# Differential attention in an encoder trunk: the score products over 64 rows each, three per component, in place of two over 128 rows

## The chip, the cores and the metric

The kernel runs on one core of a Trainium2 chip, in one launch. The metric is the device time of that core in microseconds, as the median of several executions. One more execution was taken with the hardware profiler; its trace is what is read below.

## The reference

Two layers over 512 tokens with 1024 channels, all in float32. Each layer normalizes x, multiplies it by one large input matrix and feeds two mixers: a differential attention and a gated linear recurrence (HGRN2, both directions). Their outputs are projected, gated, added, projected again and added to x; a SwiGLU block follows. What the change touches is the attention's scores:

```
def diff_attention(h_q, h_k, h_v, cos, sin, lam, norm_gain, layer):
    q = h_q.reshape(B, S, DA_HEADS, 2, DA_QK_DIM)      # 4 heads, 2 components, 64 channels
    k = h_k.reshape(B, S, DA_HEADS, 2, DA_QK_DIM)
    v = h_v.reshape(B, S, DA_HEADS, DA_V_DIM)          # 128 channels
    ...                                                # partial rotary on q and k
    def block(qi):                                     # 128 queries
        s = jnp.einsum('bqhcd,bkhcd->bhcqk', qi, k).astype(jnp.float32)
        p = jax.nn.softmax(s, axis=-1)
        w = p[:, :, 0] - lam_full * p[:, :, 1]
        return jnp.einsum('bhqk,bkhv->bqhv', w.astype(v.dtype), v)
```

So each head has two score matrices, one per component c, each a product over only 64 channels.

## The kernel before

**Precision by splitting.** Nearly every product on TensorE takes operands of type F32R, and each float32 operand x is made into two of them: hi, a copy of x cast to F32R, and lo, the rest x - hi. `split_act` (L91-92) does this with a ScalarE copy (recorded at L92) and a VectorE subtraction (recorded at L81, the line of the helper `tt`). A product is then summed from three: hi·hi, hi·lo, lo·hi (`mm3`, L209-212). Activations (helper `act`) are recorded at L78, scalar_tensor_tensor at L84.

**Stages of a layer** (L723 on): projections for the recurrence with the recurrence itself (`hgrn_head`), projections for queries (`aq`), keys (`ak`) and values, attention (L629), the second half of the gate `gb`, the projection of the recurrence's output by w_b, the gate `ga`, then the projection of the attention's output by w_a (which reads `oah`, `oal`, written by the attention), the one by w_o, and the feed-forward block. Projections run through `project_fm` and `project_tm`: weights come in by DMA (`raw`), are split into `hi` and `lo`, and 24 products (12 where the depth is 512) fill one accumulator `m`.

**Attention.** Loops over 4 heads, and in each over 4 tiles of 128 queries (`todo`, L695). Per head, `operands` (L633) turns the queries and keys by 4 + 4 TensorE transposes (L640) into the accumulators `qkt`, channels on partitions: component 0 on partitions 0 to 63, component 1 on 64 to 127. From there it makes three operands for both components:

- `q2[:, c, :]`: the hi part of component c on its own 64 partitions, the lo part on the other 64;
- `ka[:, c, :]`: the same for the keys;
- `kb[:, c, :]`: the keys with the halves exchanged, lo on the component's own partitions and hi (a cast copy) on the other.

In the profile, `q2` has the name q. That is six copies on ScalarE (L649, L652) and six subtractions on VectorE (L650, L653, recorded at L81) of 64 partitions by 512 each, a copy and a subtraction by turns, for the subtraction reads what the copy wrote.

Per tile, `exps` (L656) then needs two products per component over all 128 partitions: q2·ka gives hi·hi + lo·lo, q2·kb gives hi·lo + lo·hi (L664, L667; four products of 128x512, one accumulator `qk` per component). VectorE takes the maximum of each (L669), ScalarE the exponential with its sum (L670, recorded at L78). `weights` (L673) joins both components to one weight tile, which TensorE turns (L714, `wt`) and `split_act` splits into `wh` and `wl`. At the end of a head, `values` multiplies by the values (`ao`) and `finish` normalizes and writes `oah`, `oal`.

**What sets the order.** The program says what depends on what, and a planner in the framework lays out one fixed order per engine: where an instruction of the attention isn't ready, TensorE gets a product of a later projection instead. `urgent()` puts weight loads, splits and evacuations first. `behind(a, b)` (L94) is an order without a wait: a is placed after b in the plan. In `exps`, the first product of a head's first tile is placed behind the last subtraction of `operands` (L665). Operand tiles have one buffer each, score and side accumulators share four banks (`bank`, L107), projections have four of their own (`mbank`, L110).

Of the kernel before, what the change touches and what calls it, by code (L numbers as in the profile page):

```python
# [9 lines left out]
F32 = mybir.dt.float32  # L10
F32R = mybir.dt.float32r
# [3 lines left out]
ALU = mybir.AluOpType  # L15
# [3 lines left out]
P = 128  # L19
D = 1024  # L20
DC = D // P
T = 512
# [25 lines left out]
def kernel(  # L48
# [17 lines left out]
    PE, DVE, ACT, POOL = nc.tensor, nc.vector, nc.scalar, nc.gpsimd  # L66
# [13 lines left out]
    def tt(o, a, b, op):  # L80
        return DVE.tensor_tensor(o, a, b, op)  # L81
# [9 lines left out]
    def split_act(src, hi, lo):  # L91
        return ACT.copy(hi, src), tt(lo, src, hi.bitcast(F32), ALU.subtract)  # L92

    def behind(ins, other):  # L94

        tc.add_manual_dep(ins.ins, other.ins.name,
                          mybir.DependencyInfo(mybir.DependencyClass.NoSync, mybir.DependencyReason.DATA),
                          reason="keep the tensor engine from waiting")
# [46 lines left out]
    hl = cp.tile([P, DC, T], F32R, tag="hl", name="hl")  # L145
# [121 lines left out]
    with tc.tile_pool(name="init", bufs=1, reuse_waits="tile") as ip:  # L267
# [41 lines left out]
        with tc.issue_after(norms[-1][1].ins):  # L309
# [56 lines left out]
            for dst, quarter in ((sin, 0.0), (cos, 0.25)):  # L366
                n = ip.tile([P, 32], F32, tag="n", name="n")
# [261 lines left out]
    def attention(l, aq, ak, avh, avl, oh, ol, ap):  # L629

        def operands(h):  # L633

            half = [slice(0, 64), slice(64, 128)]
            turned = []
            for src in (aq, ak):
                pt = bank("qkt")
                for t in range(TC):
                    PE.transpose(pt[:, t * P:(t + 1) * P], src[:, t, h * P:(h + 1) * P], ident)  # L640
                turned.append(pt)
            q2 = ap.tile([P, 2, T], F32R, tag="q2", name="q2", bufs=1)
            ka = ap.tile([P, 2, T], F32R, tag="ka", name="ka", bufs=1)
            kb = ap.tile([P, 2, T], F32R, tag="kb", name="kb", bufs=1)
            for pt, dst, swapped in ((turned[0], q2, None), (turned[1], ka, kb)):
                for c in range(2):
                    own, other = half[c], half[1 - c]
                    hi = dst[own, c, :]
                    ACT.copy(hi, pt[own, :])  # L649
                    mark = tt(dst[other, c, :], pt[own, :], hi.bitcast(F32), ALU.subtract)  # L650
                    if swapped is not None:
                        ACT.copy(swapped[other, c, :], pt[own, :])  # L652
                        mark = tt(swapped[own, c, :], pt[own, :], hi.bitcast(F32), ALU.subtract)  # L653
            return (q2, ka, kb), mark

        def exps(q2, ka, kb, t, mark):  # L656

            tok = slice(t * P, (t + 1) * P)
            nm = sm.tile([P, 2], F32, tag="nm", name="nm")
            den = sm.tile([P, 2], F32, tag="den", name="den")  # L660
            e = ap.tile([P, 2, T], F32, tag="e", name="e", bufs=2)
            ps = [bank("qk") for c in range(2)]
            for c in range(2):
                mm = PE.matmul(ps[c], q2[:, c, tok], ka[:, c, :], start=True, stop=False)  # L664
                if t == 0 and c == 0:  # L665
                    behind(mm, mark)
                PE.matmul(ps[c], q2[:, c, tok], kb[:, c, :], start=False, stop=True)  # L667
            for c in range(2):
                DVE.tensor_reduce(nm[:, c:c + 1], ps[c], AX.X, ALU.max, negate=True)  # L669
                mark = act(e[:, c, :], ps[c], AF.Exp, bias=nm[:, c:c + 1], accum=den[:, c:c + 1])  # L670
            return e, den, mark

        def weights(e, den):  # L673
            DVE.reciprocal(den, den)
            tt(den, den, dcoef[:, l, :], ALU.mult)
            tsc(e[:, 1, :], e[:, 1, :], den[:, 1:2], None, ALU.mult)
            return stt(e[:, 0, :], e[:, 0, :], den[:, 0:1], e[:, 1, :], ALU.mult, ALU.add)

        def values(h, wh, wl, mark):
            po = bank("ao")  # L680
            hc = slice(h * P, (h + 1) * P)
            for s in range(TC):
                if s == 0 and mark is not None:
                    behind(PE.matmul(po, avh[:, s, hc], wh[:, s, :], start=True, stop=False), mark)
                    PE.matmul(po, avh[:, s, hc], wl[:, s, :], start=False, stop=False)
                    PE.matmul(po, avl[:, s, hc], wh[:, s, :], start=False, stop=False)
                else:
                    mm3(po, avh[:, s, hc], avl[:, s, hc], wh[:, s, :], wl[:, s, :], s == 0, s == TC - 1)
            return head_squares(po)[0]

        def finish(h, parts, mark):
            o = head_norm(*parts, dgain[:, 4 * l + h:4 * l + h + 1], mark)
            split_act(o, oh[:, h, :], ol[:, h, :])

        todo = [(h, t) for h in range(HEADS) for t in range(TC)]  # L695
        ops, mark = operands(0)
        e, den, _ = exps(*ops, 0, mark)
        for n, (h, t) in enumerate(todo):
            mark = weights(e, den)
            if t == 0:  # L700
                if h:
                    parts = values(h - 1, wh, wl, mark)
                wh = ap.tile([P, TC, T], F32R, tag="wh", name="wh", bufs=1)
                wl = ap.tile([P, TC, T], F32R, tag="wl", name="wl", bufs=1)
            elif t == 1 and h:
                finish(h - 1, parts, mark)
            w, mark = e, None
            if n + 1 < len(todo):
                if t == TC - 1:
                    ops, mark = operands(h + 1)  # L710
                e, den, mark = exps(*ops, todo[n + 1][1], mark)
            pt = bank("wt")
            for s in range(TC):
                tr = PE.transpose(pt[:, s * P:(s + 1) * P], w[:, 0, s * P:(s + 1) * P], ident)  # L714
                if mark is not None:
                    behind(tr, mark)
            tok = slice(t * P, (t + 1) * P)
            split_act(pt.rearrange("p (s c) -> p s c", c=P), wh[:, :, tok], wl[:, :, tok])
        finish(HEADS - 1, values(HEADS - 1, wh, wl, None), None)
# [3 lines left out]
    for l in range(LAYERS):  # L723
        win = w_in[l]
        an = [vecs[:, V_FFN + 8 * l + c:V_FFN + 8 * l + c + 1] for c in range(DC)]
        with ExitStack() as mix:
# [3 lines left out]
            aq = gp.tile([P, TC, 512], F32, name="aq")  # L730
            ak = gp.tile([P, TC, 512], F32, name="ak")
# [48 lines left out]
            with tc.tile_pool(name=f"merge{l}", bufs=1, reuse_waits="tile") as gm, ExitStack() as late:  # L780
# [11 lines left out]
                with tc.tile_pool(name=f"attn{l}", bufs=1, reuse_waits="tile") as ap:  # L792
# [6 lines left out]
                               k=4, ah=obh, al=obl)  # L799
# [24 lines left out]
        with tc.tile_pool(name=f"ffn{l}", bufs=2, reuse_waits="tile") as fp:  # L824
            gh = fp.tile([P, FC, T], F32R, name="gh", bufs=1)
            gl = fp.tile([P, FC, T], F32R, name="gl", bufs=1)
            for f0 in range(0, FC, 2):
# [3 lines left out]
                for f in (f0, f0 + 1):  # L831
                    c0 = slice((f - f0) * P, (f - f0 + 1) * P)
                    tmp = []
                    for raw in (rg, ru):
                        with urgent():
                            wh, wl = wsplit(raw[:, :, c0])
                        ps = mbank()
# [14 lines left out]
            if l < LAYERS - 1:  # L852
                nn = [vecs[:, V_ATT + 8 * (l + 1) + c:V_ATT + 8 * (l + 1) + c + 1] for c in range(DC)]
                for c0 in range(0, DC, 2):
                    ps = [mbank(), mbank()]
# [16 lines left out]
            else:  # L872
# [3 lines left out]
                for t in range(TC):  # L876
                    for half in range(2):
                        pt = bank("xt")
# [4 lines left out]
                ps = [[mbank(), mbank()] if t < 2 else [bank(), bank()] for t in range(TC)]  # L883
# [3 lines left out]
                for k, t, half in order:  # L887
# [6 lines left out]
                    tok, cs = slice(t * P, (t + 1) * P), slice(half * 512, (half + 1) * 512)  # L894
# [55 lines left out]
```

## Time and profile before

| | before |
|---|---|
| median of 3 runs | 1627.63 us (1626.99 to 1627.94) |
| the profiled execution, its own time | 1627.93 us |
| span of its trace | 1626.2 us |
| TensorE products (PE) busy | 1604.3 us, 7456 instructions |
| weight loads (PEld) busy | 1323.7 us |
| VectorE (DVE) busy | 1010.8 us |
| ScalarE (ACT) busy | 776.6 us |

How to read it: PE is TensorE's products, PEld its weight loads, which run beside them. Durations of products overlap: a product is recorded until its last result is out, while the next has begun. So the price of a product in a stream is the distance between two starts. A row of a timeline gives start (us from the span's start), duration (us), engine, line, operation, output<-inputs, stationary size, shape, and in brackets how long the engine stood before it and for what.

### The profile page before, as it was taken

What the parts mean: (1) busy time and instruction counts of PE and PEld (TensorE: products, weight loads), DVE (VectorE), ACT (ScalarE), POOL (GpSimd) and SP (SyncE); (2) the same over time, 40 slices, a digit from 0 to 9 for tenths busy, and PEclk for the clock granted to TensorE, in tenths of its full rate; (3) what the DMA queues carried; (4) which work ended last, traced back from release to release, by engine and by line L of the source; (5) the groups of instructions that cost most, each with busy time, mean ns of one, the idle gap of its engine ahead of it and who ended that gap; (6) DMA issues with size and microseconds to landing.
All of it is one profiled execution on the core that took longest, in us unless ns stands there. A gap on an engine that the chain in (4) does not pass through costs nothing.

```text
span 1626.2 us, 18701 instructions
## 1 busy us (share of the span) xinstructions
PE 1604.3 (99%) x7456; PEld 1323.7 (81%) x7456; DVE 1010.8 (62%) x1626; ACT 776.6 (48%) x1192; POOL 7.8 (0%) x21
## 2 busy tenths in 40 slices
PE   8999999999999999999999999999999999999998
PEld 6788888887888888888888888888878888888886
DVE  7878967887644444433368789788876444444224
ACT  5666675676433232322255567676754323233213
POOL 1000000000000000000000000000000000000000
PEclk9999999999999999999999999999999999999999
DMA  5212212221322233322332222122122233332321
GB/s 188 91 65 78 78 53 78 78 78 33 123 91 91 84 98 104 104 91 98 97 104 78 78 78 66 65 71 85 52 79 89 93 104 104 104 99 96 104 83 73
DMA packets 118823, 142.53 MB, mean 88 GB/s; under 512 B 3024, under 2 KB 101328, under 8 KB 118736
## 3 DMA queue, kind: packets, MB, share of 16 engines
q1 hardware_dynamic: 118592, 141.31, 26.8%
q8 instruction: 58, 0.95, 0.2%
q14 instruction: 29, 0.24, 0.0%
q10 hardware_dynamic: 144, 0.03, 0.0%
HBM read 139.23 MB, written 2.10 MB: 87 GB/s over the span
## 4 chain that ended last, share of the span: by engine, by line
PE 85%; DVE 9%; ACT 4%; issue 1%; DMA 0%; SPq 0%; ACTq 0%
PE m L210 24%; PE m L212 24%; PE m L211 24%; DVE fl L81 2%; DVE lo L81 2%; PE sc L551 2%; PE s L212 1%; PE s L211 1%; PE s L210 1%; PE qk L667 1%; DVE z L81 1%; PE wt L714 1%; PE po L601 1%; PE qk L664 1%; ACT hi L92 1%
## 5 line engine op out<-in xcount | busy, mean ns | idle before, releaser
L92 ACT CAST hi<-raw 128x1024 fp32r<-128x1024 f32 (+2 forms) x280 | 276.6, 989 | 612.2 <-PE m L211 469.5
L210 PE MATMUL m<-hh,hi 128*128 128x512 f32 x1216 | 476.7, 392 | 7.1 <-ACT hh L78 7.1
L211 PE MATMUL m<-hl,hi 128*128 128x512 f32 x1216 | 476.1, 392 | 0.1
L212 PE MATMUL m<-hh,lo 128*128 128x512 f32 x1216 | 476.2, 392 | 0.0
L81 DVE TENSOR_TENSOR lo<-raw,hi 128x1024 fp32r<-128x1024 f32 (+2 forms) x280 | 320.3, 1145 | 184.8 <-ACT hi L92 183.6
L210 PEld LDWEIGHTS m<-hh,hi 128*128 128x128 f32 x1216 | 229.2, 188 | 54.6 <-ACT hh L78 7.9
L211 PEld LDWEIGHTS m<-hl,hi 128*128 128x128 f32 x1216 | 228.9, 188 | 48.0 <-DVE hl L84 1.4
L212 PEld LDWEIGHTS m<-hh,lo 128*128 128x128 f32 x1216 | 229.1, 188 | 47.1
L81 DVE TENSOR_TENSOR gu<-m,rbc 128x512 f32<-128x512 f32 x88 | 60.9, 692 | 241.0 <-PE m L212 237.0
L210 PE MATMUL m<-hi,hh 128*128 128x512 f32 x256 | 101.5, 396 | 0.0
L211 PE MATMUL m<-lo,hh 128*128 128x512 f32 x256 | 100.9, 394 | 0.0
L212 PE MATMUL m<-hi,hl 128*128 128x512 f32 x256 | 100.8, 394 | 0.0
L78 ACT ACTIVATE fl<-fl 128x1024 f32<-128x1024 f32 (+1 forms) x56 | 48.4, 872 | 43.8 <-DVE fl L81 43.8
L210 PE MATMUL m<-gh,hi 128*128 128x512 f32 x176 | 68.5, 389 | 0.0
L211 PE MATMUL m<-gl,hi 128*128 128x512 f32 x176 | 68.5, 389 | 0.0
L212 PE MATMUL m<-gh,lo 128*128 128x512 f32 x176 | 68.5, 389 | 0.0
L212 PEld LDWEIGHTS m<-hi,hl 128*128 128x128 f32 x256 | 48.1, 188 | 9.6
L211 PEld LDWEIGHTS m<-lo,hh 128*128 128x128 f32 x256 | 48.2, 188 | 9.4
L210 PEld LDWEIGHTS m<-hi,hh 128*128 128x128 f32 x256 | 48.1, 188 | 9.3
L551 PEld LDWEIGHTS sc<-fl 128*128 128x128 f32 x384 | 49.0, 191 | 7.1 <-DVE fl L81 2.7
L551 PE MATMUL sc<-fl 128*128 128x128 f32 x384 | 51.4, 277 | 1.6 <-DVE fl L81 1.5
L211 PE MATMUL m<-ml,hi 128*128 128x512 f32 x128 | 49.7, 391 | 0.0
(254 smaller groups left out, 2334.3 us busy)
## 6 DMA issues: line engine op xcount, KB each, us to landing
raw<-in_w_in_dram SPq DMA_DIRECT2D x47, 1024.0 KB, 5.0
raw<-in_w_gate_dram SPq DMA_DIRECT2D x22, 1024.0 KB, 5.1
raw<-in_w_up_dram SPq DMA_DIRECT2D x22, 1024.0 KB, 5.1
raw<-in_w_down_dram SPq DMA_DIRECT2D x19, 1024.0 KB, 5.0
raw<-in_w_o_dram SPq DMA_DIRECT2D x8, 1024.0 KB, 5.0
raw<-in_w_b_dram SPq DMA_DIRECT2D x4, 1024.0 KB, 5.0
raw<-in_w_a_dram SPq DMA_DIRECT2D x4, 1024.0 KB, 4.9
raw<-in_w_down_dram SPq DMA_DIRECT2D x4, 768.0 KB, 4.3
```

The source lines that it names most:

```text
L78: return ACT.activation(o, i, func, **kw)
L81: return DVE.tensor_tensor(o, a, b, op)
L92: return ACT.copy(hi, src), tt(lo, src, hi.bitcast(F32), ALU.subtract)
L210: PE.matmul(ps, lh, rh, start=start, stop=False)
L211: PE.matmul(ps, lh, rl, start=False, stop=False)
L212: PE.matmul(ps, ll, rh, start=False, stop=stop)
L551: mm = PE.matmul(ps[:, c], K[:, c], Q[:, c], start=True, stop=True)
L601: mm = PE.matmul(po[:, tok], a, b, start=i == 0, stop=i == len(terms) - 1)
L664: mm = PE.matmul(ps[c], q2[:, c, tok], ka[:, c, :], start=True, stop=False)
L667: PE.matmul(ps[c], q2[:, c, tok], kb[:, c, :], start=False, stop=True)
L714: tr = PE.transpose(pt[:, s * P:(s + 1) * P], w[:, 0, s * P:(s + 1) * P], ident)
```

## The change

`operands` now splits the turned queries and keys once, over all 128 partitions: `qh`, `ql`, `kh`, `kl`, with two copies and two subtractions per head. `exps` takes three products per component, hi·hi, hi·lo and lo·hi, each over the 64 partitions of its component, the two components by turns. The term lo·lo is dropped. Both first products of a head's first tile are placed behind the last subtraction.

```
+        half = [slice(0, 64), slice(64, 128)]
+
         def operands(h):
-            half = [slice(0, 64), slice(64, 128)]
-            turned = []
-            for src in (aq, ak):
+            parts = []
+            for src, n in ((aq, "q"), (ak, "k")):
                 pt = bank("qkt")
                 for t in range(TC):
                     PE.transpose(pt[:, t * P:(t + 1) * P], src[:, t, h * P:(h + 1) * P], ident)
-                turned.append(pt)
-            q2 = ap.tile([P, 2, T], F32R, tag="q2", name="q2", bufs=1)
-            ka = ap.tile([P, 2, T], F32R, tag="ka", name="ka", bufs=1)
-            kb = ap.tile([P, 2, T], F32R, tag="kb", name="kb", bufs=1)
-            for pt, dst, swapped in ((turned[0], q2, None), (turned[1], ka, kb)):
-                for c in range(2):
-                    own, other = half[c], half[1 - c]
-                    hi = dst[own, c, :]
-                    ACT.copy(hi, pt[own, :])
-                    mark = tt(dst[other, c, :], pt[own, :], hi.bitcast(F32), ALU.subtract)
-                    if swapped is not None:
-                        ACT.copy(swapped[other, c, :], pt[own, :])
-                        mark = tt(swapped[own, c, :], pt[own, :], hi.bitcast(F32), ALU.subtract)
-            return (q2, ka, kb), mark
+                hi, lo = [ap.tile([P, T], F32R, tag=n + x, name=n + x, bufs=1) for x in "hl"]
+                _, mark = split_act(pt, hi, lo)
+                parts += [hi, lo]
+            return parts, mark

-        def exps(q2, ka, kb, t, mark):
+        def exps(qh, ql, kh, kl, t, mark):
...
-            for c in range(2):
-                mm = PE.matmul(ps[c], q2[:, c, tok], ka[:, c, :], start=True, stop=False)
-                if t == 0 and c == 0:
-                    behind(mm, mark)
-                PE.matmul(ps[c], q2[:, c, tok], kb[:, c, :], start=False, stop=True)
+            for i, (q, k) in enumerate(((qh, kh), (qh, kl), (ql, kh))):
+                for c in range(2):
+                    mm = PE.matmul(ps[c], q[half[c], tok], k[half[c], :], start=i == 0, stop=i == 2)
+                    if t == 0 and i == 0:
+                        behind(mm, mark)
```

## Rows read from the trace of the kernel before

**Rows 1.** The first part of the page: the span, and each engine's busy us, share of the span and instructions.

```profile
span 1626.2 us, 18701 instructions
PE 1604.3 (99%) x7456; PEld 1323.7 (81%) x7456; DVE 1010.8 (62%) x1626; ACT 776.6 (48%) x1192; POOL 7.8 (0%) x21
```

**Rows 2.** The chain of waits that ended last, as shares of the span: by engine, then by line.

```profile
PE 85%; DVE 9%; ACT 4%; issue 1%; DMA 0%; SPq 0%; ACTq 0%
PE m L210 24%; PE m L212 24%; PE m L211 24%; DVE fl L81 2%; DVE lo L81 2%; PE sc L551 2%; PE s L212 1%; PE s L211 1%; PE s L210 1%; PE qk L667 1%; DVE z L81 1%; PE wt L714 1%; PE po L601 1%; PE qk L664 1%; ACT hi L92 1%
```

**Rows 3.** The table of stretches, the attention of layer 0 and of layer 1: stretch and its length, then busy us (instructions) of PE, PEld, DVE, ACT and POOL, the granted clock of TensorE as a share, the DMA share and GB/s.

```profile
258.00:388.00 130.00, 129.74 (x613) 105.85 (x613) 107.00 (x188) 94.05 (x178) 0.00 (x0) 1.00 0.20 65
1060.00:1192.00 132.00, 131.72 (x620) 107.15 (x619) 107.04 (x189) 95.25 (x180) 0.00 (x0) 1.00 0.18 60
```

**Rows 4.** What TensorE's products waited for in the whole span: us in total, times, longest us.

```profile
PE m L212 <- DVE lo L81: 1.7, 2, 0.9
...
PE m L210 <- ACT oah L92: 1.2, 2, 0.6
...
PE qk L667 <- DVE kb L81: 0.2, 1, 0.2
```

**Rows 5.** Timeline of TensorE in the attention of layer 0: a row from the stream of products before a score block, the block's first product and the product behind the block. Between the first and the last row shown there are nine steps from start to start.

```profile
299.58 0.39 PE L211 MATMUL ao<-wl,avh 128*128 128x512 f32 x1
...
300.71 0.39 PE L664 MATMUL qk<-ka,q 128*128 128x512 f32 x1
...
301.62 0.39 PE L210 MATMUL m<-obh,hi 128*128 128x512 f32 x1
```

**Rows 6.** The score products by line: count, minimum, median and maximum duration in ns, first and last start in us, shape.

```profile
L664 PE MATMUL qk<-ka,q x64: 388/390/486, 267.8 to 1176.3; 128*128 128x512 f32 x64
L667 PE MATMUL qk<-kb,q x64: 387/391/504, 268.0 to 1176.5; 128*128 128x512 f32 x64
```

**Rows 7.** Timeline of TensorE in the recurrence: eight products of 128 columns, each with a weight load of its own, and the product behind them.

```profile
209.11 1.06 PE L551 MATMUL sc<-fl 128*128 128x128 f32 x8
209.92 0.48 PE L212 MATMUL m<-hh,lo 128*128 128x512 f32 x1
```

**Rows 8.** Timeline of TensorE at the first head's start: the third score product, the fourth, which came late, and the rest of two blocks that stand back to back.

```profile
268.25 0.39 PE L664 MATMUL qk<-ka,q 128*128 128x512 f32 x1
268.78 0.50 PE L667 MATMUL qk<-kb,q 128*128 128x512 f32 x1
269.12 0.39 PE L664 MATMUL qk<-ka,q 128*128 128x512 f32 x1
...
269.82 0.39 PE L667 MATMUL qk<-kb,q 128*128 128x512 f32 x1
```

**Rows 9.** Timeline of TensorE: four transposes of the weights, the first score product behind them, and the first product behind that block.

```profile
273.25 0.60 PE L714 MATMUL wt<-ident,e 128*128 128x128 f32 x4
273.60 0.48 PE L664 MATMUL qk<-ka,q 128*128 128x512 f32 x1
...
274.61 0.40 PE L211 MATMUL m<-hl,hi 128*128 128x512 f32 x1
```

**Rows 10.** The groups that make q2, ka and kb: count, then busy us and mean ns of one, then the idle time before them with its main releaser.

```profile
L81 DVE TENSOR_TENSOR kb<-qkt,ka 64x512 fp32r<-64x512 f32 x16 | 11.0, 689 | 3.0 <-ACT kb L652 2.6
L81 DVE TENSOR_TENSOR q<-qkt,q 64x512 fp32r<-64x512 f32 x16 | 11.0, 688 | 1.5 <-ACT q L649 1.1
L81 DVE TENSOR_TENSOR ka<-qkt,ka 64x512 fp32r<-64x512 f32 x16 | 10.9, 684 | 4.2 <-ACT ka L649 4.1
L649 ACT CAST ka<-qkt 64x512 fp32r<-64x512 f32 x16 | 9.3, 583 | 3.3 <-DVE kb L81 3.2
L649 ACT CAST q<-qkt 64x512 fp32r<-64x512 f32 x16 | 9.3, 582 | 2.2 <-DVE q L81 2.1
L652 ACT CAST kb<-qkt 64x512 fp32r<-64x512 f32 x16 | 9.3, 578 | 5.5 <-DVE ka L81 5.4
```

**Rows 11.** A copy and a subtraction of 128x512 from an accumulator, the split of the turned weights: count, minimum, median and maximum ns.

```profile
L92 ACT CAST wh<-wt x32: 576/586/600, 273.9 to 1183.9; 128x512 fp32r<-128x512 f32 x32
L81 DVE TENSOR_TENSOR wl<-wt,wh x32: 676/683/692, 274.5 to 1185.3; 128x512 fp32r<-128x512 f32 x32
```

**Rows 12.** Timeline of TensorE at the third head: the transposes of its queries, and its first score product.

```profile
315.27 0.60 PE L640 MATMUL qkt<-ident,aq 128*128 128x128 f32 x4
...
327.77 0.39 PE L664 MATMUL qk<-ka,q 128*128 128x512 f32 x1
```

**Rows 13.** Timeline of TensorE behind the last head of layer 0: the first product that reads its output.

```profile
393.56 0.97 PE L210 MATMUL m<-oah,hi 128*128 128x512 f32 x3 [0.59 <-ACT oah L92]
```

**Rows 14.** The same, some products later.

```profile
398.19 0.49 PE L212 MATMUL m<-oah,lo 128*128 128x512 f32 x1 [0.85 <-DVE lo L81]
```

**Rows 15.** What the weight load of the second score product waited for: us in total, times, longest us.

```profile
PEld qk L667 <- DVE kb L81: 3.8, 8, 0.6
```

**Rows 16.** Timeline of TensorE at the second head's start: the third score product, a projection's product and the fourth score product.

```profile
291.23 0.39 PE L664 MATMUL qk<-ka,q 128*128 128x512 f32 x1
291.45 0.39 PE L210 MATMUL m<-obh,hi 128*128 128x512 f32 x1
291.93 0.50 PE L667 MATMUL qk<-kb,q 128*128 128x512 f32 x1
```

## The prediction

> **What bounds the kernel now.** I read the busy shares first: TensorE's products are busy for 1604.3 of 1626.2 us, VectorE 62% and ScalarE 48% [rows 1]. A busy share alone doesn't say that TensorE sets the end, so I read the chain of waits next: 85% of it lies on TensorE, three quarters of the span on the three lines of the projections, and the score lines appear with 1% for L667 [rows 2]. Then the table of stretches: in the attention of layer 0 (258 to 388 us) TensorE is busy for 129.74 of 130.00 us, VectorE for 107.00, ScalarE for 94.05; layer 1 (1060 to 1192) looks the same [rows 3]. The planner fills every gap of the attention with projections. The granted clock is 1.00 in both stretches, the 2.4 GHz level. The list of TensorE's waits has 1.2 us for the last head's output (oah) and 1.7 us for a weight split (lo) at the two ends of the attention, and 0.2 us for the key operand (kb) [rows 4]. So time that TensorE spends in the attention goes into the total one for one, and work saved on ScalarE or VectorE counts only where TensorE now stands still.
>
> A 128x512 product is recorded with 0.39 us, but starts follow each other every 0.227 us: nine steps from 299.58 to 301.62, the four score products among them [rows 5]. The spacing is the price, not the duration.
>
> **The change, part by part.**
>
> *Products.* A score block (one head, one tile of 128 queries) has now four products over 128 rows; 64 + 64 records are 32 blocks [rows 6]. After, it has six over 64 rows, alternating between rows 0-63 (component 0) and rows 64-127 (component 1). No row shows a product over 64 rows. Bounds for a pair: 0.227 us if both stream at the same time, for nothing in the rows streams 512 columns faster, and 0.454 us if one follows the other. I take 0.227: the two share no array row, operand partition or accumulator bank, so the program orders nothing between them. A block then costs 3 x 0.227 = 0.681 instead of 0.907 us: 32 x 0.227 = **-7.3 us** (at the other bound 32 x 0.454 = +14.5). The Trainium skill, "TensorE: Matmul & The Clock Gate", Part 3, gives a measured 3.07 times for four row tiles, which no run here shows; if a pair got the same share of its ideal, 1.54 times, it would take 0.295 us by my estimate from that page, and the whole sum would end at +1.9 instead of -4.7.
>
> *Weight loads.* Six a block instead of four. A load is recorded with 0.19 us, but eight 128-column products, each with its load, take 209.11 to 209.92, 0.10 us each [rows 7]. Six loads need 0.6 us and fit beside 0.681; at worst the second product of a pair starts 0.10 late, once per run of 64-row products.
>
> *Going into the 64-row form and out.* No row shows it. Lower bound 0 (the array takes the next form like the next product). Upper bound from a wait: the product at 268.25 would have been followed at 268.48; the next came at 268.78, was recorded with 0.50, and its successor came 0.34 later, 0.11 over the spacing [rows 8]. If a switch lets the array run empty (0.39 - 0.227 = 0.163 us) and restarts it so (0.11), it costs 0.27, and in plus out 0.55. The nearest row is the one change of form that the kernel has: behind the 128-column transposes of e the four score products take 273.60 to 274.61, 1.01 us, 0.10 more than 0.907 [rows 9]. I take **0.10 for in and out together**. How often: 32 blocks, two of which stand back to back once per layer (268.25 to 269.82 is the second half of such a row [rows 8]), so 30 runs. At the eight heads' starts a run is cut in two, for the third pair product needs the low part of the keys, which comes last: 38 runs. 38 x 0.10 = **+3.8 us**.
>
> *Operands.* Per head ScalarE made six copies of 64x512 and VectorE six subtractions [rows 10]; after, two and two of 128x512, as wh and wl are made (586 and 683 ns) [rows 11]. Over 8 heads ScalarE sheds 8 x (6 x 0.58 - 2 x 0.586) = 18.5 us, VectorE 8 x (6 x 0.688 - 2 x 0.683) = 22.1 us. I cost this at nothing: the projections cover it today. What it can give is an earlier attention. In the third head, transposes begin at 315.27 and the first score product comes at 327.77, 12.5 us later [rows 12], for six pairs of instructions pass to and fro between two engines that also split weights. With two pairs, projections are left over when the last head ends. There TensorE stands for 0.59 us before oah's product [rows 13] and 0.85 before a split [rows 14], in each layer: 2.9 us in all [rows 4]. Bounds 0 and -2.9; I take the waits for oah alone, **-1.2 us**, since the split is another queue's matter.
>
> *The order behind the last subtraction.* Now both first products are placed behind it instead of one. The weight load of L667 waits for kb at all eight starts, 3.8 us in total, largely under earlier products [rows 15]. After, the same wait stands before the third product, with all of TensorE's queue behind it. Bounds: 0, and 8 x 0.454 = +3.6 if the two products that used to run ahead of it are missed. I take 0, for the planner puts projections there already (the one at 291.45 stands between two score products [rows 16]); they are why I count 38 runs. Transposes, exponentials, reductions and DMAs keep their number.
>
> **Sum:** -7.3 + 3.8 - 1.2 = -4.7 us, against the profiled execution: 1627.9 us, of which 1.7 lie around the span. 1627.9 - 4.7 = **1623.2 us**. That execution is 0.3 us above the median of the three runs. A difference of 0.2%, 3.3 us, is about what a measurement of this kernel can tell from no change.
>
> **The rivals.**
>
> *The switch eats the gain.* Pairs overlap, but a run costs 0.14 to 0.31 us in and out. At r per run the sum is 38r - 8.5; it is zero at r = 0.224, and the time 1627.9 us (1624.6 to 1631.2). For it: the 0.10 above is a change of form at the same 128 rows, so a real change may cost more.
>
> *The switch empties the array, both ways.* Place: the first product of every 64-row run, and the first 128-row product or transpose behind it. Price: 0.55 per run by the wait's row, 38 x 0.55 = 20.9, less 8.5: +12.4, 1640.3 us. It decides against the change from 0.31 per run. For it: a product is recorded 0.163 us longer than the spacing, so there is something to drain. Against: the products behind the transposes show no such hole. The Trainium skill, "TensorEngine Tiling (Array Packing)", Key Properties, says that changing the tiling mode drains the engine; by that rule this is the case to expect, but it gives no price, and no row here shows one.
>
> *The pairs don't overlap,* so the change does not do what it says: 32 x 0.454 - 1.2 = +13.3 us without a price for the switch, +17.1 with 0.10: 1641.2 to 1645.0. For it: no row shows two products streaming side by side. Against: the program gives them nothing in common to wait for.
>
> **How the numbers follow.** The forecast's case (overlap, up to 0.14 per run) 0.42, own range 1617.7 (no price for the switch, all 2.9 us of waits gone: -10.2) to 1624.6. Switch eats the gain 0.22; full drain 0.16; no overlap 0.20. The range takes in the first three and the lower edge of the fourth: 1617.7 to 1641.2. Faster 0.42, same 0.22, slower 0.36.
>
> **What would show it.** Right: score products with 64 rows, six a block, in pairs that start well under 0.1 us apart, pair to pair 0.227; a block in 0.8 us or less to the next product's start; the first product after it with a record near 0.39; q and k copies at 128x512, sixteen each; the last head's products sooner and its waits gone. Wrong: six products 0.227 us apart (no overlap); or a hole of 0.2 us or more before or behind each run (drain); or TensorE waiting for VectorE in the attention, whose own load is denser once heads start sooner.

## The result, and the profile after

The changed kernel takes 1630.82 us as the median of 20 runs (1629.35 to 1632.15), the kernel before on the same chips 1627.99 us (20 runs). The ratio is 1.0016, 95% interval 1.0010 to 1.0022: 2.6 us slower, 1.6 to 3.6. That lies inside the range (1617.7 to 1641.2) and less than 0.2% from the kernel before, but slower instead of faster, and 7.6 us above the forecast of 1623.2. The profiled execution took 1630.04 us with a span of 1628.3, 2.1 us more span than before.

The first part of the page, as [rows 1]: TensorE got 64 products more and 6 us more busy time, VectorE and ScalarE got lighter.

```profile
span 1628.3 us, 18758 instructions
PE 1610.2 (99%) x7520; PEld 1316.1 (81%) x7520; DVE 988.3 (61%) x1594; ACT 758.8 (47%) x1160; POOL 8.3 (1%) x21
```

The score products by line, as [rows 6] (count, minimum, median and maximum ns, first and last start, shape): 192 products over 64 rows in place of 128 over 128.

```profile
L657 PE MATMUL qk<-kh,qh x64: 386/494/502, 262.0 to 1165.5; 64*128 64x512 f32 x64
L657 PE MATMUL qk<-kl,qh x64: 387/394/502, 262.7 to 1165.9; 64*128 64x512 f32 x64
L657 PE MATMUL qk<-kh,ql x64: 384/393/395, 263.0 to 1166.1; 64*128 64x512 f32 x64
```

The operands by line, as [rows 10]: eight of each, at full height.

```profile
L92 ACT CAST qh<-qkt x8: 582/596/602, 260.0 to 1142.8; 128x512 fp32r<-128x512 f32 x8
L92 ACT CAST kh<-qkt x8: 598/606/611, 260.5 to 1143.3; 128x512 fp32r<-128x512 f32 x8
L81 DVE TENSOR_TENSOR ql<-qkt,qh x8: 680/684/686, 261.3 to 1144.6; 128x512 fp32r<-128x512 f32 x8
L81 DVE TENSOR_TENSOR kl<-qkt,kh x8: 678/680/687, 261.9 to 1145.2; 128x512 fp32r<-128x512 f32 x8
```

Timeline of TensorE around one run of 64-row products that stands between products of 512 columns over 128 rows, to be laid beside [rows 5]:

```profile
289.17 0.39 PE L212 MATMUL ao<-wh,avl 128*128 128x512 f32 x1
289.48 0.50 PE L657 MATMUL qk<-kh,qh 64*128 64x512 f32 x2
289.82 0.40 PE L657 MATMUL qk<-kl,qh 64*128 64x512 f32 x2
290.05 0.40 PE L657 MATMUL qk<-kh,ql 64*128 64x512 f32 x2
290.38 0.50 PE L210 MATMUL m<-hh,hi 128*128 128x512 f32 x1
290.72 0.40 PE L211 MATMUL m<-hl,hi 128*128 128x512 f32 x1
```

Two products stand in one row (x2): both of a pair start together, and the pairs follow at 0.34 and 0.23 us. So the pairs overlap in full. In what follows the spacing is the 0.227 us from start to start in a stream, a block is the six products of one head and one tile of 128 queries, and a run is an unbroken row of 64-row products.

Now read the four long steps, against a spacing of 0.227: 0.31 from the last 128-row product into the run, 0.34 behind the first pair, 0.33 behind the last one, 0.34 behind the first 128-row product. Each change of form costs about 0.10 us before it and 0.11 behind it, 0.42 in and out together: (0.31 + 0.34 + 0.23 + 0.33 + 0.34) - 5 x 0.227 = 0.42. The other runs between products of 512 columns read so; the five per layer behind the transposes of the weights take 0.16 us more than the same blocks of before, though they save a step of 0.227, which makes 0.39. There are 18 runs per layer: of 16 blocks two are joined, and three, at the later heads' starts, are cut in two. The joined run takes 0.40 us longer still, for its second pair waits for the low keys (`kl`).

The weight loads of the same stretch show where part of the price comes from:

```profile
288.94 0.19 PEld L212 LDWEIGHTS ao<-wh,avl 128*128 128x128 f32 x1
289.48 0.19 PEld L657 LDWEIGHTS qk<-kh,qh 64*128 64x128 f32 x2 [0.35 <-issue]
290.38 0.19 PEld L210 LDWEIGHTS m<-hh,hi 128*128 128x128 f32 x1 [0.37 <-issue]
```

In the stream a load starts a step ahead of its product (288.94 for the product at 289.17). At both changes of form it starts together with its product (289.48, 290.38), and that product is recorded with 0.50 instead of 0.39. The same is seen behind a wait in the kernel before: load and product of the late one of [rows 8] start together, at 268.78. So the 0.11 behind a change looks like the product's own load, about 0.10 by [rows 7], that no longer runs beside the product before; no experiment below takes the load apart from the change.

What went the other way is at the end of the attention, the places of [rows 13] and [rows 14]. Stretches, with length, busy us (instructions) of PE, PEld, DVE, ACT and POOL, granted clock, DMA:

```profile
388.00:400.00 12.00, 12.00 (x55) 9.94 (x54) 7.62 (x13) 5.46 (x10) 0.00 (x0) 1.00 0.26 87
1192.00:1204.00 12.00, 12.00 (x55) 9.94 (x54) 9.34 (x15) 6.56 (x11) 0.00 (x0) 1.00 0.26 87
```

TensorE is busy for all 12 us; before it was for 10.56 and 10.58. In the list of its waits `oah` and `lo` of [rows 4] are gone, and small ones at the transposes of the weights have come:

```profile
PE wt L706 <- DVE den L666: 0.3, 2, 0.2
...
PE wt L706 <- DVE e L84: 0.2, 1, 0.2
```

### The profile page after: what moved, and what is told of

Read it like the earlier page. It is cut to its first block, busy times and chain, and to the rows that moved or that the text cites. A ratio compares the mean times of both kernels' runs of the same rounds, so it can differ in the third digit from the quotient of the medians.

```text
span 1628.3 us, 18758 instructions
## 1 busy us (share of the span) xinstructions
PE 1610.2 (99%) x7520; PEld 1316.1 (81%) x7520; DVE 988.3 (61%) x1594; ACT 758.8 (47%) x1160; POOL 8.3 (1%) x21
## 4 chain that ended last, share of the span: by engine, by line
PE 85%; DVE 9%; ACT 4%; issue 1%; DMA 0%; SPq 0%; ACTq 0%
PE m L211 24%; PE m L212 24%; PE m L210 24%; DVE fl L81 2%; PE sc L551 2%; PE qk L657 2%; DVE lo L81 1%; PE s L212 1%; PE s L210 1%; PE s L211 1%; DVE z L81 1%; PE po L601 1%; PE wt L706 1%; DVE nm L661 1%; DVE cum L455 1%
## 5 line engine op out<-in xcount | busy, mean ns | idle before, releaser
L661 DVE TENSOR_REDUCE nm<-qk 128x1 f32<-128x512 f32 x64 | 42.7, 685 | 28.3 <-PE qk L657 28.3
L78 ACT ACTIVATE e<-qk,nm 128x512 f32<-128x512 f32 x64 | 43.6, 684 | 26.8 <-DVE nm L661 26.5
```

The source lines that it names most:

```text
L78: return ACT.activation(o, i, func, **kw)
```

## The experiments

Times are medians; "before" is the kernel before, timed beside that run, the ratio is of this to it. Each ratio is known to about 0.1%, so a difference between two rows with different "before", or to the changed kernel, is uncertain by some 2 us.

| run | us | before | ratio (95%) |
|---|---|---|---|
| e1_operands_only | 1621.34 | 1628.19 | 0.9960 (0.9947 to 0.9972) |
| e2_not_alternating | 1634.17 | 1628.19 | 1.0037 (1.0024 to 1.0051) |
| e3_zero_pair_64 | 1646.08 | 1628.19 | 1.0111 (1.0095 to 1.0126) |
| e4_zero_product_128 | 1649.82 | 1628.19 | 1.0129 (1.0115 to 1.0143) |
| e5_urgent_operands | 1624.98 | 1628.38 | 0.9978 (0.9969 to 0.9988) |
| e6_two_blocks | 1708.52 | 1628.38 | 1.0491 (1.0477 to 1.0505) |
| e7_zero_pair_64_late | 1642.72 | 1628.03 | 1.0090 (1.0075 to 1.0105) |
| e8_zero_product_128_late | 1643.84 | 1628.03 | 1.0093 (1.0076 to 1.0110) |
| e9_banks_6_2 | 1771.29 | 1628.03 | 1.0883 (1.0867 to 1.0899) |
| e10_two_blocks_6_2 | 1780.49 | 1628.03 | 1.0945 (1.0927 to 1.0962) |
| e15_low_keys_first | 1627.33 | 1627.98 | 0.9997 (0.9988 to 1.0006) |
| e19_before_urgent_last_first | 1627.60 | 1627.98 | 0.9996 (0.9988 to 1.0005) |
| e17_low_first_urgent | 1631.36 | 1627.98 | 1.0020 (1.0011 to 1.0029) |
| e20_zero_pair_64_unsplit | 1635.69 | 1627.98 | 1.0048 (1.0034 to 1.0061) |
| e21_zero_product_128_unsplit | 1642.34 | 1627.98 | 1.0087 (1.0073 to 1.0101) |
| e22_same_rows | 1649.95 | 1627.98 | 1.0135 (1.0119 to 1.0152) |

**Do pairs overlap because of their rows?** e22 moves component 1 to component 0's rows:

```
-  mm = PE.matmul(ps[c], q[half[c], tok], k[half[c], :], start=i == 0, stop=i == 2)
+  mm = PE.matmul(ps[c], q[half[0], tok], k[half[0], :], start=i == 0, stop=i == 2)
```

> The changed kernel with component 1's six operands taken from component 0's 64 rows (so component 1's scores are component 0's; that part of the computation is changed). Same number and shape of products, all on the same rows. Theory A (two products stream at once because they stand on different rows): three more steps of 0.227 us in each block, 32 x 0.681 = 21.8 us above the changed kernel, about 1652.5. Rival C (a 64-row product takes half the time wherever it stands): about 1631.

19.1 us above the changed kernel (1649.95 against 1630.82). Timeline of TensorE, a block behind transposes of the weights; the same block of the changed kernel stands at 268.18:

```profile
270.43 0.72 PE L657 MATMUL qk<-kh,qh 64*128 64x512 f32 x2
270.99 0.62 PE L657 MATMUL qk<-kl,qh 64*128 64x512 f32 x2
271.45 0.63 PE L657 MATMUL qk<-kh,ql 64*128 64x512 f32 x2
272.01 0.51 PE L212 MATMUL m<-hh,lo 128*128 128x512 f32 x1
```

A row of two now lasts 0.62 and pairs follow each other at 0.46, two steps; the block takes 1.58 us to the next product's start instead of 0.89, and so does every whole block of layer 0 that stands alone. Rival C is out: the gain hangs on the rows.

e2 leaves the rows and takes the alternation away:

```
-  for i, (q, k) in enumerate(((qh, kh), (qh, kl), (ql, kh))):
-      for c in range(2):
+  for c in range(2):
+      for i, (q, k) in enumerate(((qh, kh), (qh, kl), (ql, kh))):
```

> The changed kernel with the same six products, but component 0's three first, then component 1's three, so that neighbours stand on the same 64 rows, but for the one pair in the middle. Theory A (two products stream at once because they stand on different rows): five steps of 0.227 us a block in place of three, 32 x 0.454 = 14.5 us more than the changed kernel, about 1645. Rival C (a 64-row product simply takes half the time wherever it stands): no difference, about 1631.

Only 3.4 us above the changed kernel, give or take 2.4: both theories missed. The program holds the order asked for; this is TensorE's instruction list at the first head's third tile:

```
L706 MATMUL wt<-ident,e 128x128 x4
L657 MATMUL qk<-kh,qh 128x512
L657 MATMUL qk<-kl,qh 128x512
L657 MATMUL qk<-kh,ql 128x512
L657 MATMUL qk<-kh,qh 128x512
L657 MATMUL qk<-kl,qh 128x512
L657 MATMUL qk<-kh,ql 128x512
L211 MATMUL m<-hl,hi 128x512
```

and this is what the trace shows there (first fence), and at one of the two blocks of layer 0 that came out serial (second):

```profile
269.02 0.50 PE L657 MATMUL qk<-kh,qh 64*128 64x512 f32 x2
269.35 0.40 PE L657 MATMUL qk<-kl,qh 64*128 64x512 f32 x2
269.58 0.41 PE L657 MATMUL qk<-kh,ql 64*128 64x512 f32 x2
269.92 0.51 PE L211 MATMUL m<-hl,hi 128*128 128x512 f32 x1
```

```profile
298.33 0.50 PE L657 MATMUL qk<-kh,qh 64*128 64x512 f32 x1
298.67 0.39 PE L657 MATMUL qk<-kl,qh 64*128 64x512 f32 x1
298.90 0.39 PE L657 MATMUL qk<-kh,ql 64*128 64x512 f32 x1
299.00 0.50 PE L657 MATMUL qk<-kh,qh 64*128 64x512 f32 x1
299.34 0.39 PE L657 MATMUL qk<-kl,qh 64*128 64x512 f32 x1
299.58 0.39 PE L657 MATMUL qk<-kh,ql 64*128 64x512 f32 x1
```

In the first, three products of component 1 that stand behind three of component 0 start with them. In the second, component 1 starts when component 0 is at its third. What held it there was not tried, but the trace points to it: ScalarE is still at the second exponential of the tile before, which reads one of the four accumulators that the blocks share. This is the last instruction of it, the read of its sum:

```profile
298.75 0.20 ACT L78 ACTIVATION_READ_ACCUMULATOR e<-qk,nm 128x1 f32 x1
```

It ends at 298.95, and component 1 starts at 299.00. In the other three serial blocks the start follows the same end by 0.05 to 0.06 us, so component 1 seems to have waited for its accumulator. There are two per layer, 0.65 us longer each: 2.6 of the 3.4 us.

**What do the lighter operands give back?** e1 takes the operands of the change and the amount of products of before:

```
+  for c in range(2):
+      mm = PE.matmul(ps[c], qh[:, tok], kh[:, :], start=True, stop=False)
...
+      PE.matmul(ps[c], ql[:, tok], kl[:, :], start=False, stop=True)
```

> The operands of the changed kernel (two copies and two subtractions per head) with four products of 128 rows per block, as before: qh by kh and ql by kl over the full height, so each score mixes both components (that part of the computation is changed, its amount on TensorE is that of before). No 64-row form is left. Theory A (the lighter operands give back the waits at the heads' starts and at the attention's end, and the switches between forms take it away again): 4 to 5.5 us less than before, 1622.5 to 1624. Rival B (the operands are covered and give nothing; the pairs' gain and a small switch cost nearly cancel): as before, 1627 to 1629.

1621.34 us, 0.9960: 6.5 us less than before (4.6 to 8.6), a little more than theory A asked. The stretches of both attentions have no idle time of TensorE left (before: 140.29 of 142 and 142.29 of 144):

```profile
258.00:400.00 142.00, 142.00 (x669) 116.38 (x668) 107.83 (x192) 91.69 (x176) 0.00 (x0) 1.00 0.19 66
...
1060.00:1204.00 144.00, 144.00 (x674) 118.00 (x673) 110.66 (x196) 92.08 (x175) 0.00 (x0) 1.00 0.20 66
```

e5 gives the kernel before earlier heads without taking work away:

```
-  ops, mark = operands(h + 1)
+  with urgent():
+      ops, mark = operands(h + 1)
```

> The kernel before, all its work unchanged, with the operands of each head marked urgent for the planner, so that they no longer queue behind weight splits and evacuations of the projections. It gives the earlier heads of the changed kernel without its lighter operands and without 64-row products. Theory A (what the change won back is the time at which the heads start): the waits at the attention's end shrink, 1 to 3 us less than before, 1625 to 1627. Rival E (the amount of ScalarE and VectorE work sets the attention's pace, not the heads' starts): as before, 1627 to 1629.

1624.98 us, 0.9978 (0.9969 to 0.9988): 3.6 us less than before by the ratio, a little beyond what theory A expected, and less than the changed kernel by 5.8. The waits at the attention's end are gone here too, those for kb at the heads' starts are not (3.5 us of weight loads, as 3.8 in [rows 15]). So earlier heads by themselves win about half of what e1 won. They are not as early as in the changed kernel: the third head's first scores come at 320.27 us here, at 310.04 there and at 327.77 before [rows 12]. How the rest divides between still earlier heads and the lighter work was not tested. e5 is faster than both kernels.

e19 adds to e5 the products that read kb first, to get rid of the rest:

```
+  for c in (1, 0):
+      mm = PE.matmul(ps[c], q2[:, c, tok], kb[:, c, :], start=True, stop=False)
...
+      PE.matmul(ps[c], q2[:, c, tok], ka[:, c, :], start=False, stop=True)
```

> The kernel before with urgent operands, and with the product that reads the last-made key operand (component 1, kb) first in each block, so that TensorE is not given a block whose last operand is still to come. It aims at the waits at the heads' starts that were left when the operands alone were urgent. Theory A (waits at the heads' starts, about 0.4 us in each of eight): 2 to 3.5 us less than with urgent operands alone, 1621.5 to 1623.5, below both kernels. Rival E (those waits only move): 1624 to 1626, as with urgent operands alone.

1627.60 us: nothing gained over before, 2.6 us lost against e5. Rival E is nearer, and it too was too kind: the weight loads still wait 4.1 us for kb, now before the whole block, and no product runs ahead of the wait.

e17 does the same to the changed kernel with the low keys first (e15, below):

> The changed kernel with the low keys first (30 runs) and the operands urgent for the planner as well. Theory A (the operands' relief is already had in the changed kernel, its heads start early enough): within 1.5 us of the kernel with the low keys first, 1626 to 1629. Rival (the heads' starts still hold TensorE up): 2 us or more less, below 1625.5.

1631.36 us, 4.0 above e15, give or take 2: worse than either theory. TensorE now waits 2.4 us for VectorE at the transposes of the weights (0.7 in e15), and in 258 to 388 it is busy for 128.77 us instead of 129.59. Heads that start sooner are not good by themselves; in this kernel they brought TensorE to the weights before VectorE had them.

**What does a change of form cost?** A product of zero weights is put into each block between the second and third pair; it adds nothing to the scores. e3 adds it as a pair in the 64-row form, e4 as one product over 128 rows:

```
+  if i == 1:
+      for c in range(2):      # e3
+          PE.matmul(ps[c], zero_r[half[c], :], kh[half[c], :], start=False, stop=False)
...
+  if i == 1:                  # e4
+      PE.matmul(ps[0], zero_r, kh, start=False, stop=False)
```

> The changed kernel with one more pair of 64-row products in each block, between the second and the third pair, with weights of zero, accumulating into the same banks. One more step in the same form: theory A 32 x 0.227 = 7.3 us more than the changed kernel, about 1638. Rival D (the six weight loads are what the block waits for): more than that, each load 0.1 us and not hidden, 32 x 0.2 on top, about 1644.

> The same place and the same streaming time as the zero pair, but as one product of zero weights over 128 rows: one more step and one more change out of the 64-row form and back per block. Theory A (0.21 us for each change of form, 0.42 for both): 7.3 + 32 x 0.42 = 20.7 us more than the changed kernel, about 1651.5, 13.4 above the zero pair. Rival B (0.10 for both, as predicted): 7.3 + 3.2, about 1641.

e4 came out at +19.0 us over the changed kernel, near theory A. e3 came out at +15.3, twice what theory A asked, and the difference of the two, 3.7 us, is near rival B's 3.2 by its size, but says nothing, for the two kernels wait differently. The trace says why: an undisturbed block of e3 is 0.23 longer than one of the change (1.13 against 0.90), as expected, so rival D is out; but TensorE waits 2.4 us for the low keys and 3.0 for VectorE at the transposes, and is busy for 139.11 of 142 us from 258 to 400, where e4 is busy throughout. e7 and e8 are the same two with `t > 0`:

> The zero pair in the 64-row form again, now only in the 24 blocks that don't start a head, for in the first try TensorE stood at the heads' starts for the low keys and for weights, which blurred the comparison. Theory A and B both: 24 x 0.227 = 5.4 us more than the changed kernel, about 1636.

> The zero product over 128 rows in the same 24 blocks: the same streaming time, and 24 more changes out of the 64-row form and back. Theory A (0.42 us for both): 24 x 0.42 = 10.1 us above the zero pair of the same blocks, about 1646. Rival B (0.10): 2.4 us above it, about 1638.5.

1642.72 and 1643.84: the same blur, the first with 3.3 us of waits at the transposes and 2.4 for the low keys, the second with none of either. Why the zero pair brings these waits and the zero product does not was not found. The total again shows 1.1 us where the blocks show 0.39 each (1.52 against 1.13).

So the base was mended first. e15 changes the order of the products, so that a head's first block starts with the operand that is made last and isn't cut:

```
-  for i, (q, k) in enumerate(((qh, kh), (qh, kl), (ql, kh))):
+  for i, (q, k) in enumerate(((qh, kl), (qh, kh), (ql, kh))):
```

> The changed kernel with the same six products per block in another order: hi by the low keys first, then hi by hi, then lo by hi. The low keys are made last, so a head's first block need not be cut in two while it waits for them: 30 runs of 64-row products in place of 36, nothing else changed. Theory A (0.42 us per run): 6 x 0.42 = 2.5 us less than the changed kernel, 1628 to 1629. Rival B (0.10 per run): 0.6 us less, 1630 to 1630.8.

1627.33 us, 3.5 below the changed kernel (3.1 by the ratios, give or take 1.8), with 30 runs and not a product less: theory A. Its price gives 2.5 us; another 0.8 is read at the joined run of each layer, which takes 1.59 us to the next product here and 1.99 in the changed kernel, where its second pair waits for the low keys. The result is level with before (0.9997, 0.9988 to 1.0006). On it, the zero pair and the zero product in 24 blocks once more:

> The kernel with the low keys first and one more pair of 64-row products with zero weights in the 24 blocks that don't start a head: 24 x 0.227 = 5.4 us above the kernel with the low keys first, about 1632.8; more if TensorE runs into VectorE's weights at the transposes again.

> The same with one zero product over 128 rows in place of the zero pair. Theory A (about 0.4 us out of the 64-row form and back): 24 x 0.62 = 14.9 us above the kernel with the low keys first, about 1642, 9 to 10 above the zero pair. Rival B (0.10): about 1635, 2.4 above the zero pair.

e21 is 15.0 us above e15 (14.9 expected), e20 8.4 (5.4 expected). Stretches of the two attentions in e20, then in e21:

```profile
258.00:388.00 130.00, 128.33 (x640) 98.29 (x639) 95.03 (x172) 82.65 (x160) 0.00 (x0) 1.00 0.19 64
...
1060.00:1192.00 132.00, 130.27 (x648) 99.91 (x647) 96.39 (x174) 83.45 (x161) 0.00 (x0) 1.00 0.19 64
```

```profile
258.00:388.00 130.00, 129.79 (x614) 95.16 (x613) 95.13 (x170) 81.40 (x159) 0.00 (x0) 1.00 0.20 64
...
1060.00:1192.00 132.00, 131.79 (x622) 96.76 (x621) 96.94 (x174) 80.94 (x155) 0.00 (x0) 1.00 0.19 64
```

e20 holds 3.0 us of idle time that e21 doesn't. The measured difference is 6.65 us, which by itself lies between the two theories; with the 3.0 it is 9.6, or 0.40 us per change out and back, where theory A said 9 to 10 and rival B 2.4. Without e20, e21's 15.0 us over e15, less 24 steps of 0.227, give 0.40 as well. The timeline of a block of e21 shows the same:

```profile
274.41 0.50 PE L657 MATMUL qk<-kl,qh 64*128 64x512 f32 x2
274.75 0.40 PE L657 MATMUL qk<-kh,qh 64*128 64x512 f32 x2
275.07 0.50 PE L661 MATMUL qk<-kh,zero_r 128*128 128x512 f32 x1
275.50 0.50 PE L657 MATMUL qk<-kh,ql 64*128 64x512 f32 x2
275.93 0.50 PE L212 MATMUL m<-hh,lo 128*128 128x512 f32 x1
```

Between two forms the step is 0.43 (275.07 to 275.50), 0.20 over the spacing, and each product behind a change is recorded with 0.50.

**Fewer runs by two tiles at once.** e6 computes the scores of two query tiles in one run of twelve products, the second tile's accumulators from the projections' banks; e10 does it with six banks for the attention, and e9 is the changed kernel with those banks.

```
+  ps = [[pool("qk") for c in range(2)] for pool in (bank, mbank)]        # e6
...
+  pm = ctx.enter_context(tc.tile_pool(name="pmain", bufs=2, space=PSUM))    # e9, e10
+  pside = ctx.enter_context(tc.tile_pool(name="pside", bufs=6, space=PSUM))
```

> The changed kernel with the score blocks of two query tiles in one run of twelve 64-row products (the second tile's accumulators come from the projections' four banks, the exponentials have three buffers). Half as many runs, 16 to 24 in place of 36. Theory A (0.42 us per run): at least 12 runs fewer, 5 us or more less than the changed kernel, 1623 to 1626, under the kernel before as well, if the four banks and the buffers put no new wait in. Rival B (0.10 per run): 1.2 to 2 us less, 1629 to 1630.

> The changed kernel with the eight accumulator banks shared out as six for the attention and the recurrence and two for the projections, in place of four and four (token-major projections take two of each). It is the base of the next kernel and tells of the change by itself nothing. Runs of 64-row products stay 36. Every theory: within 2 us of the changed kernel, 1629 to 1633, if two banks keep the projections going.

> Score blocks of two query tiles in one run, with the six and two banks, so that the projections keep banks of their own, which they lacked in the first try with two blocks. 20 runs of 64-row products in place of 36, the same products. Theory A (0.42 us per run): 16 x 0.42 = 6.7 us less than the kernel with six and two banks, about 1624. Rival B (0.10 per run): 1.6 us less, about 1629.

All three say nothing of the price. In e6 the projections' banks were taken, so TensorE had less to fill the attention with: it is busy for 118.19 of 142 us in 258 to 400, and the granted clock falls from 1.00 to 0.89 there, part of it at the 1.2 GHz level (0.60 in 274 to 282 us, after TensorE was busy for 3.15 of the 8 us before).

```profile
258.00:400.00 142.00, 118.19 (x524) 87.04 (x523) 89.54 (x165) 71.51 (x144) 0.00 (x0) 0.89 0.14 45
```

Two banks don't keep the projections going either: e9 is 143 us slower than the kernel before, and from 20 to 258 us TensorE is busy for 200.17 of 238 us, at a granted clock of 0.86, instead of 234.76 at 1.00. On that base e10 was 9 us slower again. Two tiles per run with eight banks is left open.

## Why the prediction was wrong

*What bounds the kernel* held: what e21 and e22 added to TensorE's blocks came out in the total (15.0 us for 14.9; 19.1 for some 21), and ScalarE and VectorE counted only through TensorE's waits.

*Products* (-7.3 us) held: three steps of 0.227 in place of four, shown by the pairs and by e22. The 3.07 times for four row tiles of the Trainium skill, "TensorE: Matmul & The Clock Gate", Part 3, did not carry over as a share: a pair here loses nothing.

*Weight loads* held inside a run: both products of a pair start together, also with eight loads in a block in 29 of e3's 36 runs (in seven the second comes 0.03 to 0.33 us late). At a run's two ends the load does not run ahead, which is part of the next term.

*Going into the 64-row form and out* is the step that failed. I took 0.10 us from the transposes' row and reckoned 38 runs, +3.8; the runs are 36 and cost 0.42, +15.1. The bounds (0 and 0.55) held; the choice between them was wrong, because [rows 9] is no change between 128 and 64 rows: the 0.10 there is a single long step behind short products. The nearer row was the restart in [rows 8], whose 0.11 and 0.50 stand behind each change too, and which I had put in as the extreme. The rule weighed with the second rival is from the Trainium skill, "TensorEngine Tiling (Array Packing)", Key Properties: a change of tiling mode drains the engine. The trace agrees that a change costs time on TensorE, 0.10 us before it and 0.11 behind it; the part before it is less than the 0.163 by which a product's record exceeds the spacing. Whether that is a drain can't be told from the records, for the profile models the ends of products; the price above is read from their starts.

*Operands* failed the other way. I took -1.2 us, with -2.9 as the bound; e1 measured -6.5 (-8.6 to -4.6). The bound took the waits of the list [rows 4] as they stand. Read as steps between starts, the trace of before holds more. These are the products ahead of the waits of [rows 13] and [rows 14]:

```profile
392.58 0.39 PE L212 MATMUL m<-oah,lo 128*128 128x512 f32 x1
...
396.94 0.40 PE L211 MATMUL m<-oal,hi 128*128 128x512 f32 x1
```

From 392.58 to 393.56 and from 396.94 to 398.19 is 0.75 and 1.02 us over the spacing, and the step behind each is 0.11 longer: 2.0 us per layer, 4.0 in all instead of 2.9. At each head's start the score product that waits for `kb` comes 0.12 to 0.31 us late [rows 8] [rows 16], with 0.11 behind it: 2.6 us in all, of which I had counted nothing, for I called the 3.8 us of [rows 15] largely covered. Of both together, 6.6 us, e1's trace has 0.3 left.

*The order behind the last subtraction* (0) was near in size but not harmless: besides the six extra runs, which stand in the term above, the two joined runs, one at each layer's first head, stand 0.40 us each for the low keys, 0.8 in all (0.3 of it is left at the same place in e1 too). e15, which only changes the order of the products, wins back both.

The sum with measured terms: -7.3 + 15.1 - 6.5 + 0.5 = +1.8 us, the 0.5 being what the joined runs stand beyond e1, against 2.6 measured (1.6 to 3.6). The rest lies within e1's interval and wasn't resolved further. That the time came within 0.5% of the forecast is luck: the price of the runs was put 11.3 us too low and the operands' gain 5.3 us too low, and the one hid the other. By its time this is the first rival (the switch eats the gain, 1624.6 to 1631.2, where 38 x 0.14 gives 1624.7 for the lower edge), by its price the second one (it decided from 0.31 us a run). That it did not reach 1640 is owed in about equal parts to the price (15.1 us instead of 20.9) and to the operands (-6.5 instead of -1.2), and no case of the prediction had both. The third rival fell. Of the signs named beforehand as right, the pairs came, but a block takes 0.89 to 0.90 us instead of 0.8 or less, and the first product behind it is recorded with 0.50 instead of 0.39; the hole of 0.2 us named for a drain did not come either.

## What to carry to other kernels

A smaller tile of the array pays only per run: count how often the stream goes into the other form and back (0.42 us here, nearly two products of 512 columns), and keep runs long and unsplit by putting the product with the last-made operand first. Where an engine is the bound and yet stands now and then for data, reckon what its waits cost with the restart behind them and with those of its weight loads; making the same operands earlier (e5) was worth more here than the new form. After each change look where the wait went: earlier heads helped the kernel before (e5) and hurt the changed one with the low keys first (e17 against e15).

## What the runs showed of the hardware that was not expected

- Products over different 64 rows don't keep the program's order among each other: in e2, three of rows 64 to 127 that stand behind three of rows 0 to 63 start with them, in all but two blocks of layer 0 (0.90 us a block against 1.53 and 1.57 in those two, where the later three start 0.05 us behind the end of ScalarE's exponential of the tile before).
- Two such products at once cost nothing more than one: 0.23 us per pair, 0.46 when both are on the same rows (e22).
- The step of a 128-row product between two 64-row pairs is 0.43 us where form changes on both sides of it (e21), 0.20 over the spacing; per change, 0.10 of it lies before and 0.11 behind.
- Weight loads, which in a stream of 512 columns start 0.227 us ahead of their product, start together with it at every change between 128 and 64 rows, in and out, as they do behind a wait (289.48 and 290.38 in the changed kernel, 268.78 in the kernel before).
